# A two-layer decoder trunk on one core: output projection in one sum per chunk, sink-head biases on GpSimd, transposed probabilities of two key chunks in one bank

## The chip, the core and the metric

The kernel runs on one core of a Trainium2 chip. A core has five engines with their own instruction queues, each worked off strictly in order: TensorE (PE in the profile; its weight loads, PEld, overlap the matmuls), VectorE (DVE), ScalarE (ACT), GpSimd (POOL) and SyncE (SP, which only issues DMAs here). Engines wait for each other by semaphores. Matmul results land in PSUM, of which the kernel has eight banks of 128 x 512 float32; everything else lies in SBUF. The metric is the device time of one execution in microseconds (us).

## The reference

The input x is 512 tokens of 1024 numbers. All arithmetic is float32. Layer 0 mixes two kinds of attention heads, layer 1 has one kind, and each layer ends in a squared-ReLU MLP:

```python
def sliding_window_sink_attention(q, k, v, sinks, slopes):        # heads "B" of layer 0
    ...
    dist = qpos[:, None] - kpos[None, :] + BLOCK
    valid = ((dist >= 0) & (dist < WINDOW_B))[None] & (abs_k >= 0)[:, None, :]
    s = s - slope_kg * dist.astype(jnp.float32)
    s = jnp.where(valid[None, :, None, None], s, -jnp.inf)
    m = jnp.maximum(jnp.max(s, axis=-1, keepdims=True), sink)
    p = jnp.exp(s - m)
    den = jnp.sum(p, axis=-1) + jnp.exp(sink - m)[..., 0]
    ...
def even_mixer(...):
    ...
    y = jnp.concatenate([a_out.reshape(bsz, seq, -1), b_out.reshape(bsz, seq, -1)], axis=-1)
    return jnp.einsum("bse,ed->bsd", y, w_out)

def reference(x, ...):
    for layer in range(DEPTH):
        h = rms_norm(x, g_mix[layer])
        x = x + (even_mixer(h, ...) if layer % 2 == 0 else odd_mixer(h, ...))
        x = x + squared_relu_mlp(rms_norm(x, g_mlp[layer]), w_up[layer], w_down[layer])
    return x
```

Heads "A" of layer 0 (eight) mix three dilated windows; heads "B" (eight, in groups of four over two key heads) see the last 128 tokens and have a learned sink; heads "C" of layer 1 (sixteen) are causal with a forget gate. Head size is 64. After attention, the 16 heads side by side (1024 numbers per token) are multiplied by w_out (1024 x 1024) and added to x.

## The kernel before

**Tiling.** Float32 products are made of three fast ones: each operand is split into a high part and the rest (`split`, lines 147 to 156: high part by ACT, POOL or DVE, rest by DVE or POOL), and `mm3` (lines 163 to 169) multiplies high by high, low by high and high by low into one bank. Weights are loaded 512 KB at a time by SP into one of four buffers `wraw` (`load_w`, line 179) and then split into `whi` and `wlo`. The eight banks are two groups of four in rotation: `pA` for projections (`pj`) and the output projection (`op`), `pB` for all that attention does: transposed queries and keys (`qkT`), scores (`S`), transposed probabilities (`PT`) and head outputs (`O`). A buffer or bank is taken again only when its last reader is done, so a late reader makes a later writer wait.

**One head.** `scores` (lines 325 to 374) makes for each of the four blocks of 128 queries the scores of the keys in reach (PE, lines 348 and 349), adds the bias and takes the row's maximum (DVE, line 362), takes exponentials with their sum (ACT, line 365), the reciprocal of the sum (DVE, line 368), and scales the row (POOL, line 373, for three blocks, ACT, line 370, for the fourth). The bias of an A or B head is one DVE instruction per head, distance times slope plus a mask (lines 329 and 331; the tables `dist`, `lt`, `lb` are made at the start by `make_tables`, line 698). In a B head the sink goes as one more column into the row of probabilities (POOL copy, line 360). `values` (lines 376 to 410) transposes the probabilities by key chunk c = 0 to 3 on PE (line 385): chunk c holds the query blocks that see it, four, three, two and one of them for A and C heads, two, two, two and one for B heads. Each chunk has its own bank, from which ACT takes the high part (line 397) and DVE the rest (line 398). Chunks 2 and 3 share a tile `PT3`, in which 128 columns are zero so that chunk 3 can be multiplied at a width of 256. Then eight matmuls add the head's output up in one bank `O` (line 405), ACT and DVE add its two halves to `yf` (lines 408, 409), and behind every second head the pair's 128 rows are split into a tile y (line 156).

**What sets the order.** `run(att, n_att, dense, n_dense, lead)` (line 453) weaves a generator of attention steps with a generator of dense work, in proportion to `n_att` and `n_dense`. An attention step is one query block of `scores` or one step of `values` of the head before it; `values` had a step per key chunk and one for the output, so five. The tile framework then orders the instructions of each engine by what they wait for. Layer 0 has three such stages, at lines 566 to 569: two pairs of A heads with the projections for the B heads; the eight B heads with the projections for the other A heads; the other A heads with the output projection. Pairs are numbered as y tiles: A heads 0 to 3, B heads 4 to 7. Layer 1 has four stages (lines 596 to 599), the last with its output projection.

**The output projection** (`out_part`, lines 485 to 507) went over the eight chunks of 128 output columns with the pairs known first ([0, 1, 4, 5] in layer 0, twelve matmuls a chunk), added each bank to the residual (DVE, line 504, `acc<-op,xl`), then over the eight chunks again with the next pairs ([6, 7], six matmuls a chunk), adding to `acc` (`acc<-op,acc`), and a third time with the last two pairs inside the MLP's start (`finish`).

## Time and profile before

| | |
|---|---|
| three runs | 1161.77, 1161.94, 1162.87 us; median 1161.94 |
| the profiled execution | 1160.99 us, of which 1159.2 us from the first to the last instruction (the span) |
| busy, share of the span | PE 99%, PEld 84%, DVE 75%, ACT 56%, POOL 17% |
| granted TensorE clock | 1.000 |
| stages of layer 0 | heads A with projections about 45 to 100 us, heads B about 100 to 155, heads A with output projection about 155 to 215 |
| attention of layer 1 | about 605 to 812 us, the output projection from about 765 |
| MLPs | about 215 to 600 us and 812 us to the end |

The profile gives an instruction's start and end. Matmuls are pipelined: one starts before the end of the one ahead, and their ends are modelled, so PE looks busy almost all the time and short waits hide in it. A better reading is how many matmuls start in a stretch against how many could. A row of a group reads: line, engine, operation, what is written from what, shape, count, then busy us and mean ns of one, then idle time before them and what ended it.

### The profile page before, as it was taken

To read this page: it belongs to the slowest core of one execution; us is meant where nothing else is said; L and a number is where in the kernel's file an instruction comes from. 1 tells how busy PE (TensorE), PEld (TensorE's weight loads), DVE (VectorE), ACT (ScalarE), POOL (GpSimd) and SP (SyncE) were. 2 spreads that over 40 slices of the span, in tenths; PEclk is the share of its full clock that TensorE was granted. 3 is DMA by queue.
4 is the path that set the end of the run, shared out by engine and by line. 5 is a ranking of instruction groups with operands and counts; after the bars stand their busy time and mean duration, and the time that the engine had idled before them with its cause. 6 is when DMAs were issued, how large, how long until landed. Compare 5 with 4: busy or idle time off the path is not lost.

```text
span 1159.2 us, 17365 instructions
## 1 busy us (share of the span) xinstructions
PE 1141.9 (99%) x6228; PEld 977.8 (84%) x6228; DVE 873.0 (75%) x1865; ACT 645.2 (56%) x1342; POOL 198.1 (17%) x292
## 2 busy tenths in 40 slices
PE   9999999999999999999999999999999999999998
PEld 7887887888989988988988888888888888888887
DVE  7878899969868857855647877778858759669676
ACT  7555867655545455444335685655756455465452
POOL 0445434100000000000255545332100000000000
PEclk9999999999999999999999999999999999999999
DMA  8432114232333332433443433343420722523403
GB/s 288 131 91 74 55 38 146 75 108 91 93 108 92 112 105 76 123 96 111 147 128 109 110 101 98 111 129 117 161 86 18 230 80 67 188 73 111 147 34 109
DMA packets 94695, 126.57 MB, mean 109 GB/s; under 512 B 5888, under 2 KB 66304, under 8 KB 94608
## 3 DMA queue, kind: packets, MB, share of 16 engines
q1 hardware_dynamic: 93568, 123.29, 34.7%
q10 hardware_dynamic: 1040, 2.16, 0.5%
q8 instruction: 49, 0.80, 0.3%
q14 instruction: 38, 0.31, 0.1%
HBM read 114.39 MB, written 4.23 MB: 102 GB/s over the span
## 4 chain that ended last, share of the span: by engine, by line
PE 84%; DVE 8%; DMA 3%; ACT 2%; issue 2%; POOL 1%; SPq 0%; POOLq 0%; DVEq 0%; ACTq 0%
PE up L165 10%; PE up L169 10%; PE up L168 10%; PE pj L236 4%; PE pj L234 4%; PE pj L235 4%; PE O L405 3%; PE PT L385 2%; PE op L169 2%; PE op L165 2%; PE op L168 2%; PE Y L1045 2%; PE Y L1042 2%; PE Y L1044 2%; PE Y L1091 1%
## 5 line engine op out<-in xcount | busy, mean ns | idle before, releaser
L165 PE MATMUL up<-xin,whi 128*128 128x512 f32 x512 | 200.6, 392 | 0.0
L169 PE MATMUL up<-xin,whi 128*128 128x512 f32 x512 | 199.4, 389 | 0.0
L168 PE MATMUL up<-xin,wlo 128*128 128x512 f32 x512 | 199.3, 389 | 0.0
L791 ACT CAST whi<-wraw 128x512 fp32r<-128x512 f32 x228 | 139.2, 619 | 105.1 <-PE up L169 47.7
L792 DVE TENSOR_TENSOR wlo<-wraw,whi 128x512 fp32r<-128x512 f32 x228 | 151.6, 685 | 50.9 <-ACT whi L791 50.7
L169 PEld LDWEIGHTS up<-xin,whi 128*128 128x128 f32 x512 | 96.1, 188 | 20.1
L168 PEld LDWEIGHTS up<-xin,wlo 128*128 128x128 f32 x512 | 96.2, 188 | 19.9 <-issue 0.2
L165 PEld LDWEIGHTS up<-xin,whi 128*128 128x128 f32 x512 | 96.2, 188 | 19.6 <-issue 0.2
L365 ACT ACTIVATE P<-P,negm 128x128 f32<-128x128 f32 (+5 forms) x128 | 69.5, 543 | 42.7 <-DVE negm L362 40.3
L973 ACT ACTIVATE u<-up 128x512 f32<-128x512 f32 x64 | 38.3, 598 | 90.9 <-PE up L169 90.9
L234 PE MATMUL pj<-whi,hn 128*128 128x512 f32 (+2 forms) x256 | 88.7, 347 | 0.0
L236 PE MATMUL pj<-whi,hn 128*128 128x512 f32 (+2 forms) x256 | 87.0, 340 | 0.0
L235 PE MATMUL pj<-wlo,hn 128*128 128x512 f32 (+2 forms) x256 | 86.9, 339 | 0.0
L153 POOL TENSOR_SCALAR whi<-wraw 128x512 fp32r<-128x512 f32 x88 | 59.7, 680 | 158.7 <-PE pj L236 137.6
L812 DVE TENSOR_TENSOR t<-u 128x256 f32<-128x256 f32 x56 | 23.2, 423 | 62.8 <-ACT u L1116 61.1
L156 POOL TENSOR_TENSOR wlo<-wraw,whi 128x512 fp32r<-128x512 f32 x48 | 63.8, 1332 | 21.4 <-ACT whi L151 18.9
L156 DVE TENSOR_TENSOR wlo<-wraw,whi 128x512 fp32r<-128x512 f32 (+1 forms) x71 | 49.0, 698 | 18.6 <-POOL whi L153 15.1
L373 POOL TENSOR_SCALAR P<-P,rden 128x256 f32<-128x256 f32 (+2 forms) x96 | 48.0, 503 | 82.8 <-DVE rden L368 77.2
L397 ACT CAST PT<-PT 128x256 fp32r<-128x256 f32 (+3 forms) x128 | 48.9, 403 | 20.3 <-PE PT L385 19.4
L362 DVE CUSTOM_DVE_ANT_0 P<-S,bias 128x128 f32<-128x128 f32 (+1 forms) x96 | 45.7, 484 | 17.4 <-PE S L351 11.8
L791 ACT CAST whi<-mraw 128x512 fp32r<-128x512 f32 x64 | 38.8, 620 | 33.1 <-DVE mraw L902 14.4
L385 PE MATMUL PT<-ident,P 128*128 128x128 f32 x296 | 53.4, 276 | 2.4 <-DVE negm L362 1.4
(241 smaller groups left out, 3083.5 us busy)
## 6 DMA issues: line engine op xcount, KB each, us to landing
wraw<-in_w_up SPq DMA_DIRECT2D x64, 512.0 KB, 4.3
wraw<-in_w_down SPq DMA_DIRECT2D x56, 512.0 KB, 3.8
wraw<-in_w_in_odd SPq DMA_DIRECT2D x22, 512.0 KB, 3.8
wraw<-in_w_in_even SPq DMA_DIRECT2D x17, 512.0 KB, 5.0
mraw<-in_w_down SPq DMA_DIRECT2D x16, 512.0 KB, 4.7
K<-K SPq DMA_DIRECT2D x26, 256.0 KB, 2.9
bias<-csp SPq DMA_DIRECT2D x16, 256.0 KB, 3.3
wraw<-in_w_out_odd SPq DMA_DIRECT2D x8, 512.0 KB, 3.7
```

Source lines behind the costliest of these rows:

```text
L153: nc.gpsimd.tensor_scalar(dst_h, src, 1.0, 1.0, op0=OP.mult, op1=OP.mult)
L156: in_order((nc.gpsimd if lo == "pool" else nc.vector).tensor_sub(dst_l, src, dst_h.bitcast(F32)))
L165: m = nc.tensor.matmul(o, wh, xh, start=start, stop=False, skip_group_check=more)
L168: nc.tensor.matmul(o, wl, xh, start=False, stop=False, skip_group_check=more)
L169: nc.tensor.matmul(o, wh, xl, start=False, stop=stop, skip_group_check=more)
L234: nc.tensor.matmul(o, xh, hi[:, :n], start=k == 0, stop=False)
L235: nc.tensor.matmul(o, xh, lo[:, :n], start=False, stop=False)
L236: nc.tensor.matmul(o, xl, hi[:, :n], start=False, stop=k == DC - 1)
L365: nc.scalar.activation(p[:, :ne], p[:, :ne], AF.Exp, scale=-1.0, bias=negm[:, i:i + 1], accum_out=den[:, i:i + 1])
L385: nc.tensor.transpose(pt[:, (i - c) * P:(i - c + 1) * P], pr[i][:, kb * P:(kb + 1) * P], ident)
L791: sca(nc.scalar.copy(dst_h, src))
L792: late.append(lambda: vec(nc.vector.tensor_sub(dst_l, src, dst_h.bitcast(F32))))
```

## The change

Three edits, and new step counts for `run` where the number of steps changed.

First, `out_two` takes the place of the first two passes of the output projection: a chunk's bank takes the products of the first pairs (`a`), stays open, takes those of the next pairs (`b`), and is then added once to the residual. `OUT_ORDER` writes the order out by hand: four chunks' `a` first, with the loads of the residual (`x`) between, then their `b`, then chunk by chunk. The four `pA` banks are all open at the start of this.

Second, the masks of the B heads go into one float32 table of distances `db` (distance, and 1e30 where a key is out of reach), and a head's bias is that table times a number, by GpSimd.

Third, `values` puts two key chunks into one bank: (0, 1) and (3, 2) for B heads, 512 and 384 columns; 0, 1 and (3, 2) for A and C heads, 512, 384 and 384 columns. One ACT and one DVE instruction serve the two. The transposes and the matmuls are the same ones.

```diff
+OUT_ORDER = (("a", 0), ("a", 1), ("a", 2), ("x", 0), ("a", 3), ("b", 0), ("x", 2), ("b", 1), ("b", 2), ("b", 3), ("a", 4),
+             ("x", 4), ("b", 4), ("a", 5), ("b", 5), ("a", 6), ("x", 6), ("b", 6), ("a", 7), ("b", 7))
...
-NB = 86
+NB = 69
...
                 elif kind == "b":
-                    nc.vector.scalar_tensor_tensor(bias[:, :256], dist[:, 256:], -8.0 * float(slopes[h]), lb,
-                                                   op0=OP.mult, op1=OP.add)
+                    nc.gpsimd.tensor_scalar(bias[:, :256], db, -8.0 * float(slopes[h]), 1.0, op0=OP.mult, op1=OP.mult)
...
-                pts = []
-                for c in range(NT):
+                pts = {}
+
+                for cs in (((0, 1), (3, 2)) if kind == "b" else ((0,), (1,), (3, 2))):
                     pt = bank("pB", "PT")
...
-                    nc.scalar.copy(dst[:, 0], pt[:, :n])
-                    nc.vector.tensor_sub(dst[:, 1], pt[:, :n], dst[:, 0].bitcast(F32))
-                    pts.append((rhs, cols))
+                    nc.scalar.copy(d[:, 0], pt[:, :n])
+                    nc.vector.tensor_sub(d[:, 1], pt[:, :n], d[:, 0].bitcast(F32))
                     yield
...
+            def out_two(pa, pb):
...
+                for what, c in OUT_ORDER:
+                    if what == "x":
+                        xls[c // 2] = wp.tile([P, 2, 512], F32, tag="wraw", bufs=RAW, name="xl")
+                        nc.sync.dma_start(xls[c // 2], residual(li, c // 2))
+                        accs.append(acc_slot(f"acc{li}_{c // 2}"))
+                        continue
+                    if what == "a":
+                        os[c] = bank("pA", "op")
+                        product(c, pa, True, False)
+                        yield 32 * len(pa)
+                    else:
+                        product(c, pb, False, True)
+                        nc.vector.tensor_add(accs[c // 2][:, c % 2], os[c], xls[c // 2][:, c % 2])
+                        yield 32 * len(pb)
...
-                run(att_a(0), 32, chain(kv_b(), project([(1536, 2048)], qk_use("b", 8))), 768, LEADS[0])
+                run(att_a(0), 30, chain(kv_b(), project([(1536, 2048)], qk_use("b", 8))), 768, LEADS[0])
                 run(att_b(), NB, chain(qk_a(1), v_a(1)), 768, LEADS[1])
-                run(chain(att_a(1), last_values()), 38, chain(out_part([0, 1, 4, 5], True),
-                                                              out_part([6, 7], False), ahead([2, 3])), 1536, LEADS[2])
+                run(chain(att_a(1), last_values()), 33, chain(out_two([0, 1, 4, 5], [6, 7]), ahead([2, 3])), 1536, LEADS[2])
...
-                    run(att_c(g), 36, chain(qk_c(g + 1), v_c(g + 1)), 768, LEADS[3 + g])
-                run(chain(att_c(3), last_values()), 42, chain(out_part([0, 1, 2, 3], True),
-                                                              out_part([4, 5], False), ahead([6, 7])), 1536, LEADS[6])
+                    run(att_c(g), 32, chain(qk_c(g + 1), v_c(g + 1)), 768, LEADS[3 + g])
+                run(chain(att_c(3), last_values()), 37, chain(out_two([0, 1, 2, 3], [4, 5]), ahead([6, 7])), 1536, LEADS[6])
...
-        in_order(nc.vector.tensor_scalar(f[:, :256], dist[:, 256:], 0.0, -8.0 * BIG, op0=OP.is_lt, op1=OP.mult))
+        in_order(nc.vector.tensor_scalar(f[:, :256], dist[:, 256:], 0.0, BIG, op0=OP.is_lt, op1=OP.mult))
         yield
-        in_order(nc.vector.tensor_scalar(lb, dist[:, 256:], 128.0, -8.0 * BIG, op0=OP.is_ge, op1=OP.mult))
+        in_order(nc.vector.tensor_scalar(db, dist[:, 256:], 128.0, BIG, op0=OP.is_ge, op1=OP.mult))
         yield
-        in_order(nc.vector.tensor_add(lb, lb, f[:, :256]))
+        in_order(nc.vector.tensor_add(db, db, f[:, :256]))
+        yield
+        in_order(nc.vector.tensor_add(db, db, dist[:, 256:]))
         yield
```

The instructions also stand in another order. Three places matter below; numbers in names tell tiles of one kind apart, and line numbers are those of each kernel's own file (in the changed one the subtraction from a `PT` bank is line 404, the sum into `yf` line 414, the sum into `acc` line 518, the bias on GpSimd line 333).

**DVE at the end of the B heads**, where the sixth B head's output is summed into `yf` and the queries of the other A heads are normalised (`qk<-qk,rs`). Before:

```order
L331 SCALAR_TENSOR_TENSOR bias_2011<-dist_100,lb_102 128x256
L135 SCALAR_TENSOR_TENSOR rs_1862<-rsq_1868,rsq_1867 128x32 [waits DVE_49]
L161 SCALAR_TENSOR_TENSOR v0_103<-pj0_1885,rcol_95,v0_103 128x4x64
L275 TENSOR_TENSOR qk_1842<-qk_1842,rs_1862 128x512 [waits DVE_49]
L275 TENSOR_TENSOR qk_1843<-qk_1843,rs_1862 128x512
L409 TENSOR_TENSOR yf_1647<-O_1997,yf_1647 64x512 [waits Activation_49]
L362 ISA P_2019,negm_2013<-S_2016,bias_2011,nsink_86 128x128 [waits Pool_49]
```

In the changed kernel:

```order
L414 TENSOR_TENSOR yf_1615<-O_1944,yf_1615 64x512 [waits Activation_49]
L135 SCALAR_TENSOR_TENSOR rsq_1811<-ssv_1804,rsq_1810 128x32 [waits DVE_49]
L369 RECIPROCAL rden_1962<-den_1961 128x1 [waits Activation_49]
L363 ISA P_1987,negm_1960<-S_1984,bias_1958,nsink_86 128x256 [waits PE_49]
L363 ISA negm_1960 128x1
L136 TENSOR_TENSOR rsq_1811<-rsq_1811,rsq_1810 128x32 [waits DVE_49]
L404 TENSOR_TENSOR PT_1998<-PT_1993,PT_1998 128x512 [waits Activation_49]
L137 SCALAR_TENSOR_TENSOR rs_1805<-rsq_1811,rsq_1810 128x32 [waits DVE_49]
L158 TENSOR_TENSOR y0_6_1955<-yf_1615,y0_6_1955 128x512 [waits Activation_49]
L277 TENSOR_TENSOR qk_1785<-qk_1785,rs_1805 128x512 [waits DVE_49]
L277 TENSOR_TENSOR qk_1786<-qk_1786,rs_1805 128x512
```

The sum into `yf` now stands nine rows ahead of the two normalisations, and not behind them.

**DVE behind the second pair of A heads' keys**, in the stage with the output projection. Before, between the pair's last key and its first scores (`P<-S`):

```order
L301 TENSOR_TENSOR Q_2447<-qkT_2442,Q_2447 64x512 [waits Activation_49]
L329 SCALAR_TENSOR_TENSOR bias_2597<-dist_100,lt_101 128x512 [waits DVE_49]
L161 SCALAR_TENSOR_TENSOR K_2461<-qkT_2452,gg_85,K_2461 64x512 [waits DMAHW6_49,Activation_49]
L504 TENSOR_TENSOR acc0_2_2427<-op_2487,xl_2425 128x512 [waits PE_49]
L156 TENSOR_TENSOR wlo_2629<-wraw_2626,whi_2628 128x512 [waits DMAHW3_49,Pool_49]
L156 TENSOR_TENSOR wlo_2633<-wraw_2626,whi_2632 128x512 [waits Pool_49]
L504 TENSOR_TENSOR acc0_3_2545<-op_2546,xl_2543 128x512 [waits DMAHW2_49,PE_49]
L362 ISA P_2474,negm_2468<-S_2471,bias_2466 128x128 [waits PE_49]
```

In the changed kernel:

```order
L163 SCALAR_TENSOR_TENSOR K_2352<-qkT_2347,gg_85,K_2352 64x512 [waits DMAHW0_49,Activation_49]
L303 TENSOR_TENSOR Q_2342<-qkT_2337,Q_2342 64x512 [waits Activation_49]
L518 TENSOR_TENSOR acc0_0_2306<-op_2169,xl_2304 128x512 [waits PE_49]
L163 SCALAR_TENSOR_TENSOR K_2356<-qkT_2347,gg_85,K_2356 64x512 [waits DMAHW6_49,Activation_49]
L518 TENSOR_TENSOR acc0_0_2306<-op_2228,xl_2304 128x512 [waits PE_49]
L518 TENSOR_TENSOR acc0_1_2393<-op_2257,xl_2391 128x512 [waits DMAHW3_49,PE_49]
L518 TENSOR_TENSOR acc0_1_2393<-op_2307,xl_2391 128x512 [waits PE_49]
L363 ISA P_2386,negm_2380<-S_2383,bias_2378 128x128 [waits PE_49]
```

Two splits of weights (`wlo`) are gone from in front of the scores, and the sums into `acc` are four instead of two.

**GpSimd in the B heads.** Before:

```order
L360 COPY P_1928<-nsink_86 128x1 [waits PE_49,Pool_49]
L156 TENSOR_TENSOR wlo_2337<-wraw_2329,whi_2336 128x512 [waits Pool_49]
L373 TENSOR_SCALAR P_1754<-P_1754,rden_1750 128x128 [waits DVE_49]
L373 TENSOR_SCALAR P_1763<-P_1763,rden_1750 128x256 [waits DVE_49]
L360 COPY P_1955<-nsink_86 128x1 [waits PE_49]
L360 COPY P_1970<-nsink_86 128x1 [waits PE_49]
L373 TENSOR_SCALAR P_1790<-P_1790,rden_1750 128x256 [waits DVE_49]
```

In the changed kernel:

```order
L374 TENSOR_SCALAR P_1715<-P_1715,rden_1711 128x128 [waits DVE_49]
L361 COPY P_1911<-nsink_86 128x1 [waits PE_49,Pool_49]
L361 COPY P_1938<-nsink_86 128x1 [waits PE_49,Activation_49]
L374 TENSOR_SCALAR P_1724<-P_1724,rden_1711 128x256 [waits DVE_49]
L158 TENSOR_TENSOR wlo_2262<-wraw_2258,whi_2261 128x512 [waits DMAHW5_49,Activation_49]
L333 TENSOR_SCALAR bias_1958<-db_102 128x256 [waits DVE_49]
L374 TENSOR_SCALAR P_1753<-P_1753,rden_1711 128x256 [waits DVE_49]
```

A head's bias now stands between the scalings of the rows of the head before it, here behind a split of output weights that waits for its load (DMAHW5) and for ScalarE.

More of the change, by code (lines that the diff above doesn't have):

```diff
@@ L376, in values, with blocks @@
             def values(pr, kind, V, vs, yf, j):
[L378 to L379 removed]
+                def blocks(c):
+                    return [i for i in range(c, NT) if kind != "b" or i <= c + 1]
+                pts = {}
+                for cs in (((0, 1), (3, 2)) if kind == "b" else ((0,), (1,), (3, 2))):
                     pt = bank("pB", "PT")
[L381 to L399 removed]
@@ new lines, in values @@
+                    n = 0
+                    for c in cs:
+                        for i in blocks(c):
+                            kb = c - (max(i - 1, 0) if kind == "b" else 0)
+                            nc.tensor.transpose(pt[:, n:n + P], pr[i][:, kb * P:(kb + 1) * P], ident)
+                            n += P
+                    if cs == (3, 2):
+                        d = p3[:, :, P:]
+                        pts[3] = p3[:, :, :256], slice(256, 512)
+                        pts[2] = p3[:, :, 256:], slice(256, 512)
+                    else:
+                        d = ap.tile([P, 2, 512 - cs[0] * P], F32R, tag=f"PT{cs[0]}", bufs=1, name="PT")
+                        o = 0
+                        for c in cs:
+                            m = len(blocks(c)) * P
+                            pts[c] = d[:, :, o:o + m], slice(c * P, c * P + m)
+                            o += m
@@ L483, in out_weights, with product, out_last @@
                 return load_w(runs, w, np_, PAT_OP)
-            def out_part(pairs, first, finish=None, tiles=None):
+            def out_two(pa, pb):
+                ws, xls, os = {}, {}, {}
+                def product(c, pairs, start, stop):
+                    w = 1024 // len(pairs)
+                    c0 = c // (w // P) * (w // P)
+                    if (len(pairs), c0) not in ws:
+                        ws[len(pairs), c0] = out_weights(pairs, c0)
+                    cw = slice((c - c0) * P, (c - c0 + 1) * P)
+                    for kk, n in enumerate(pairs):
+                        hi, lo = ws[len(pairs), c0][kk]
+                        mm3(os[c], hi[:, cw], lo[:, cw], ys[n][:, 0], ys[n][:, 1], start and kk == 0,
+                            stop and kk == len(pairs) - 1)
+                for what, c in OUT_ORDER:
[12 more added lines that the diff above has]
+                        yield 32 * len(pb)
+            def out_last(pairs, finish, tiles):
                 np_ = len(pairs)
                 w = 1024 // np_
-                tiles = tiles or {}
                 for c in range(DC):
@@ L495, in out_part @@
                     cw = slice(e * P, (e + 1) * P)
-                    if first and c % 2 == 0:
-                        xl = wp.tile([P, 2, 512], F32, tag="wraw", bufs=RAW, name="xl")
-                        nc.sync.dma_start(xl, residual(li, c // 2))
-                        accs.append(acc_slot(f"acc{li}_{c // 2}"))
                     o = bank("pA", "op")
@@ L503, in out_part @@
                     a = accs[c // 2][:, c % 2]
-                    nc.vector.tensor_add(a, o, xl[:, c % 2] if first else a)
-                    if finish is not None:
-                        finish(c, a)
+                    nc.vector.tensor_add(a, o, a)
+                    finish(c, a)
                     yield 32 * np_
@@ L696, in start, with make_tables @@
             pass
-    def make_tables(ap, dist, lt, lb):
+    def make_tables(ap, dist, lt, db):
         def scratch(dt, tag, name):
```

23 lines of the change are left out of this document (4 added, 19 removed).

## The prediction

> **What bounds the kernel now.** I read the page's head first, then busy time by stage, then what PE waited for, and the rows around each of those waits.
>
> ```profile
> PE 1141.9 (99%) x6228; PEld 977.8 (84%) x6228; DVE 873.0 (75%) x1865; ACT 645.2 (56%) x1342; POOL 198.1 (17%) x292
> ```
>
> Busy time by stage (columns: the stretch, its length, busy us and instructions of PE, PEld, DVE, ACT, POOL, the clock, DMA):
>
> ```profile
> 45.00:100.00 55.00, 54.27 (x313) 46.31 (x312) 42.94 (x131) 32.14 (x82) 24.43 (x38) 1.00 0.31 90
> 100.00:155.00 55.00, 52.84 (x350) 45.35 (x350) 48.67 (x163) 41.95 (x122) 29.08 (x64) 1.00 0.18 53
> 155.00:215.00 60.00, 56.20 (x306) 46.77 (x305) 54.39 (x136) 37.12 (x93) 21.27 (x29) 1.00 0.36 106
> 605.00:765.00 160.00, 158.13 (x994) 136.51 (x993) 124.00 (x344) 98.72 (x235) 74.62 (x96) 1.00 0.37 106
> 900.00:928.90 28.90, 28.90 (x129) 23.96 (x128) 20.53 (x33) 12.63 (x23) 0.00 (x0) 1.00 0.72 229
> ```
>
> PE is the bound; the change keeps every matmul, so only its waits can be won. The last row, an MLP stretch at full flow, holds some 128 matmuls of 512 columns: 28.90 / 128 = 0.226 us each. One is shown longer than that:
>
> ```profile
> L168 PE MATMUL up<-xin,wlo 128*128 128x512 f32 x512 | 199.3, 389 | 0.0
> ```
>
> So a wait below about 0.16 us does not show, and one that shows is about 0.16 us longer than shown (0.389 - 0.226). In 100 to 215 us PE stands idle for 2.16 + 3.80 us, and there DVE is busy 103.1 of 115 us, 90%. In layer 1's attention PE idles 1.9 us. What PE waited for from 45 to 215 us (in total, times, longest):
>
> ```profile
> PE PT L385 <- DVE negm L362: 1.4, 1, 1.4
> PE S L348 <- DVE yf L409: 1.2, 1, 1.2
> PE qkT L290 <- DVE qk L275: 1.2, 2, 0.7
> PE qkT L290 <- POOL qk L275: 1.1, 2, 0.5
> PE PT L385 <- POOL P L373: 0.9, 1, 0.9
> PE O L405 <- DVE PT L398: 0.4, 2, 0.3
> PE op L169 <- DVE y L156: 0.3, 1, 0.3
> PE S L348 <- DVE Q L301: 0.2, 1, 0.2
> PE O L405 <- ACT PT L397: 0.2, 1, 0.2
> ```
>
> Together 6.9 us, nearly all behind DVE. The two kinds at `qkT` (2.3 us) are the normalisation of queries; its instructions stay, and I leave them.
>
> **The change part by part.** The costs by shape (whole run):
>
> ```profile
> L397 ACT CAST PT<-PT 128x512 fp32r<-128x512 f32 x24 | 14.0, 584 | 5.9 <-PE PT L385 5.6
> L398 DVE TENSOR_TENSOR PT<-PT 128x512 fp32r<-128x512 f32 x24 | 16.4, 685 | 0.4 <-ACT PT L397 0.4
> L398 DVE TENSOR_TENSOR PT<-PT 128x384 fp32r<-128x384 f32 x24 | 13.2, 550 | 0.4 <-ACT PT L397 0.2
> L398 DVE TENSOR_TENSOR PT<-PT,PT 128x256 fp32r<-128x256 f32 x32 | 13.2, 414 | 0.1
> L398 DVE TENSOR_TENSOR PT<-PT,PT 128x128 fp32r<-128x128 f32 x32 | 8.9, 279 | 1.7 <-ACT PT L397 1.7
> L331 DVE SCALAR_TENSOR_TENSOR bias<-dist,lb 128x256 f32<-128x256 f16 x8 | 3.7, 461 | 0.0
> L504 DVE TENSOR_TENSOR acc<-op,acc 128x512 f32<-128x512 f32 x32 | 21.7, 682 | 2.9 <-PE op L169 2.6
> L373 POOL TENSOR_SCALAR P<-P,rden 128x256 f32<-128x256 f32 x40 | 20.9, 524 | 10.9 <-DVE rden L368 10.5
> ```
>
> Two chunks per bank: an A or C head takes 0.414 + 0.279 - 0.550 = 0.143 us less of DVE, a B head 3 x 0.414 + 0.279 - 0.685 - 0.550 = 0.286 us less. ACT is relieved in the same way; at 56% busy nothing of the sum is put on it. One sum: of the 32 `acc<-op,acc`, 16 fall away (8 per layer, 0.682 us each, 5.5 us of DVE per layer). Biases: 8 x 0.461 = 3.7 us leave DVE. In 100 to 155 us DVE thus loses 2.3 + 3.7 = 6.0 of 48.67 us, in 155 to 215 us 5.5 + 0.6 = 6.1 of 54.39: 12%. None of it is PE time as such; it counts where PE waited behind DVE. Four waits are in places that the new order alters.
>
> *The sum into `yf`.* The rows of DVE and PE around 156 us:
>
> ```profile
> 153.26 2.81 DVE L275 TENSOR_TENSOR qk<-qk,rs 128x512 f32<-128x512 f32 x2
> 156.10 0.68 DVE L409 TENSOR_TENSOR yf<-O,yf 64x512 f32<-64x512 f32 x1
> 156.84 0.39 PE L348 MATMUL S<-K,Q 128*128 128x256 f32 x1 [1.23 <-DVE yf L409]
> ```
>
> A score needs the bank that `yf` still reads, and `yf` stands behind two normalisations. By the new order it stands nine rows ahead of them: 1.2 + 0.16 = 1.4 us go. Late next is the second half of `PT`, behind the normalisations now; PE has 20 projection matmuls between the two parts of that head's output to fill it.
>
> *The scores of the second pair.* DVE first, then PE:
>
> ```profile
> 187.43 2.12 DVE L156 TENSOR_TENSOR wlo<-wraw,whi 128x512 fp32r<-128x512 f32 x2
> 189.48 0.68 DVE L504 TENSOR_TENSOR acc<-op,xl 128x512 f32<-128x512 f32 x1
> 190.08 0.27 DVE L362 CUSTOM_DVE_ANT_0 P<-S,bias 128x128 f32<-128x128 f32 x1
> 190.41 0.55 PE L385 MATMUL PT<-ident,P 128*128 128x128 f32 x3 [1.41 <-DVE negm L362]
> ```
>
> The transposes need a bank that the first score still holds, and its maximum stands behind two splits and a sum, 2.7 us of DVE. The splits no longer stand there; the last of the four sums there needs 0.68 us after its matmuls, which the head's own score matmuls cover in good part. 1.4 + 0.16 = 1.6 us go.
>
> *The weights of the second quarter.* GpSimd:
>
> ```profile
> 172.53 1.13 POOL L153 TENSOR_SCALAR whi<-wraw 128x512 fp32r<-128x512 f32 x1 [1.35 <-DMA wraw<-in_w_out_even]
> 173.63 0.93 POOL L373 TENSOR_SCALAR P<-P,rden 128x384 f32<-128x384 f32 x2
> ```
>
> GpSimd waited for a load of output weights, with a head's scalings queued behind; that is PE's 0.9 us at the scaling. `OUT_ORDER` asks for these weights before the first residual, so one 512 KB load earlier on SP: 1.0 us goes.
>
> *The last y.* The output projection waited 0.3 us for the pair split last; with `b` of the last chunk and more matmuls on the pair before it, 13 instead of 10 matmuls stand in between, 0.7 us more. 0.3 + 0.16 = 0.5 us go.
>
> The short waits at `O` and `Q` (0.8 us shown, four times 0.16 hidden, and, as an estimate, as much again too short to show) come to 2.9 us; with 12% less DVE I take a quarter, 0.7 us. Layer 1's attention has 1.9 us shown, and of that
>
> ```profile
> PE S L348 <- DMA K<-K: 1.7, 2, 1.2
> ...
> K<-K SPq DMA_DIRECT2D x26, 256.0 KB, 2.9
> ```
>
> is the copy of a key's halves, which stays; from the rest and from 45 to 100 us I take 0.5 us.
>
> What is added. (1) Eight biases on GpSimd: the scaling of the same size, 0.524 us, eight times 4.2 us in a stage where it is busy 29.08 of 55. At nothing, since a head's bias is made while the head before it is at work; without that cover, up to 0.524 us each. (2) One more addition of 256 columns in the tables, 0.414 us at most, in the first 45 us: 0.2. (3) In the first A head of the output stage no matmuls of the projection stand between the seven transposes, the scores and the first output product: between the first four transposes and that product PE has three transposes and two scores, about 1.1 us, against 0.584 + 0.685 us of ACT and DVE and a maximum on DVE before it: between 0 and 1.6, taken 0.8 for being nearer such a wait than not. (4) Between a pair's keys and its first scores lie 26 and 24 output matmuls (5.9 and 5.4 us) where about 27 and 24 lay; the copy takes 2.9 us after DVE's part: 0 to 1.2, taken 0.3.
>
> Sum: 1.4 + 1.6 + 1.0 + 0.5 + 0.7 + 0.5 = 5.7 off, 0.2 + 0.8 + 0.3 = 1.3 on, net 4.4 us off. The profiled execution took 1160.99 us (1159.2 of span and 1.8 around it), 0.95 under the median of the runs: 1156.6 there, 1157.5 against 1161.94.
>
> [...] DVE from 45 to 215 us, and the same split in the MLPs, where GpSimd is idle:
>
> ```profile
> L156 DVE TENSOR_TENSOR wlo<-wraw,whi 128x512 fp32r<-128x512 f32 x17 | 13.0, 767 | 1.3 <-POOL whi L153 1.2
> L156 DVE TENSOR_TENSOR y<-yf,y 128x512 fp32r<-128x512 f32 x8 | 6.3, 782 | 0.8 <-ACT y L151 0.7
> L275 DVE TENSOR_TENSOR qk<-qk,rs 128x512 f32<-128x512 f32 x4 | 4.9, 1276 | 0.0
> L792 DVE TENSOR_TENSOR wlo<-wraw,whi 128x512 fp32r<-128x512 f32 x228 | 151.6, 685 | 50.9 <-ACT whi L791 50.7
> ```
>
> Beside a working GpSimd these take 17 x 0.082 + 8 x 0.097 + 4 x 0.59 = 4.5 us longer, over 74.8 us of GpSimd: 0.06 us per us, so 0.25 us of DVE for 4.2 us more. [...]
>
> **The rivals.**
>
> *Waits come back elsewhere* (1161): each wait removed shows the next dependency; on a PE that stalls only some 10 us from 45 to 215 us the scheduler's new order may hold as many. For it: at (3) and (4) I can name two. Against: DVE, the common releaser, has 12% less to do. 4.4 us off, 3.5 back.
>
> [...]
>
> *GpSimd's queue becomes the late one* (1165, the slower side): in the B heads the biases stand between sink copies, scalings and a split that waits for its load; a head's scalings then come late, and its transposes with them. It decides when most of the eight push a scaling that PE waits for: 8 x 0.524 = 4.2 on, and the DVE gain of that stage gone: 1161.94 + 4.2 - 1.0. For it: PE's 0.9 us behind a GpSimd scaling at 173 us. Against: GpSimd is busy 53% there.
>
> **How the numbers follow.** Forecast 1157.5: 0.64; waits come back 0.18; DVE held off 0.06; GpSimd's queue 0.12. A measurement here tells 0.2%, 2.3 us, from no change. Faster takes nearly all of the forecast and a sixth of the two middle cases: 0.66; same 0.21; slower 0.13. The forecast's own range is 1153 to 1159.6: the 5.7 with no addition and 3 us more of waits that do not show, or the 5.7 with the additions' upper ends (0.4 + 1.6 + 1.2 = 3.2). The whole range, 1151 to 1164, takes in the middle cases and leaves most of the last out.
>
> **What would show it.** Right: no wait of PE for `yf` or for the maximum above 0.5 us in 100 to 215 us, DVE about 12 us less busy up to 215 us, the MLP starting some 4 us earlier, layer 1 within 1 us of before. Wrong: a wait of PE for `O` behind `PT` or for `K` of 1 us or more in the output stage; GpSimd as releaser of transposes in the B heads; `wlo` on DVE well above 767 ns.

## The result and the profile after

The changed kernel takes 1172.89 us (median; 1171.91 to 1174.94) against 1162.01 us (1161.77 to 1162.87): a ratio of 1.0098, 95% interval 1.0086 to 1.0109. It is 10.9 us slower; the forecast was 4.4 us faster, and the range of the prediction (1151 to 1164) does not hold it.

The profiled execution took 1171.91 us with a span of 1170.1. Its busy line, then what PE waited for in the whole span (in total, times, longest):

```profile
PE 1147.0 (98%) x6228; PEld 977.7 (84%) x6228; DVE 860.4 (74%) x1802; ACT 643.9 (55%) x1302; POOL 204.9 (18%) x300
```

```profile
PE O L410 <- DVE PT L404: 4.8, 6, 1.7
PE S L349 <- DMA K<-K: 2.9, 3, 1.2
PE qkT L292 <- DVE qk L277: 2.2, 2, 1.6
```

The matmuls are the same 6228, and DVE is busy 12.6 us less, on 63 instructions fewer. What is new is the first wait: the output product for the rest of the transposed probabilities, 4.8 us where it was 0.4.

**Where the time went.** A comparison by clock time does not line the two kernels up, so I lined them up by work: every matmul is counted at its undisturbed start-to-start time in these traces (0.227 us for 512 columns, 0.176 for 384, 0.120 for 256, 0.108 for a transpose), and for an amount of work the table gives the time at which a kernel gets there, less that of before. A rising number is lost PE time, and the place where it rises is the place of the loss. All kernels of the experiments stand in it but two sets of leads (further, small steps). The six added matmuls of one kernel count as work here, so that kernel loses 1.4 us more than its row says.

| work done, us (before is there at) | 80 (89) | 110 (124) | 140 (158) | 200 (222) | 650 (679) | 690 (720) | 730 (760) | 800 (832) |
|---|---|---|---|---|---|---|---|---|
| the changed kernel | 2.0 | 4.2 | 3.9 | 4.5 | 5.7 | 7.0 | 9.4 | 10.9 |
| biases alone | 0.9 | 0.8 | 2.5 | 0.4 | 0.3 | 0.3 | 0.3 | 0.2 |
| one sum alone | 0.3 | 0.3 | 0.3 | 0.0 | 0.0 | 0.0 | 0.1 | 2.6 |
| pairs alone | 0.4 | 2.7 | 3.0 | 1.9 | 3.2 | 4.5 | 8.3 | 8.4 |
| pairs undone | 0.7 | 0.7 | 2.3 | 1.4 | 2.2 | 2.2 | 2.2 | 4.0 |
| pairs, empty steps behind | 0.5 | 3.1 | 2.6 | 5.4 | 5.9 | 6.9 | 6.6 | 6.7 |
| pairs, empty steps ahead | 1.4 | 3.3 | 1.9 | 1.3 | 2.2 | 3.1 | 4.9 | 5.0 |
| two chunks a step | 1.1 | 1.3 | 0.3 | 0.1 | 1.0 | 0.7 | 5.1 | 5.4 |
| six more matmuls | 3.1 | 3.7 | 3.2 | 3.0 | 5.9 | 7.2 | 11.1 | 12.7 |
| changed, leads u | 1.9 | 1.6 | 3.4 | 0.1 | 3.8 | 4.9 | 4.9 | 5.4 |
| changed, leads v | 0.7 | 2.6 | 3.4 | 1.0 | 3.1 | 3.5 | 6.3 | 7.1 |
| changed, leads w | 2.2 | 2.2 | 2.6 | 2.8 | 10.2 | 11.1 | 11.3 | 15.7 |
| before, leads 0.03 up | 1.3 | 0.6 | 1.8 | 1.1 | 2.5 | 3.1 | 8.2 | 9.0 |
| before, leads 0.03 down | -0.1 | 1.0 | 4.4 | 4.6 | 10.9 | 11.0 | 14.6 | 14.8 |
| changed, leads by stage | 0.5 | 0.2 | 1.4 | -0.3 | 1.2 | 2.2 | 2.2 | 3.0 |
| changed, leads by stage, 2nd | 1.1 | 2.0 | 3.2 | 1.7 | 2.6 | 3.4 | 3.4 | 3.9 |

So the changed kernel loses 4.5 us in layer 0, 1.9 of it on the way into the B heads (work 80 to 100), nothing in the MLPs, and 6.4 us in layer 1's attention, 2.2 of it around one wait of its third stage. These two places show what happens in the others too.

*The third stage of layer 1*, around 759 us. All engines, rows in between left out:

```profile
755.29 1.29 POOL L158 TENSOR_TENSOR wlo<-wraw,whi 128x512 fp32r<-128x512 f32 x1
...
755.33 1.29 DVE L133 TENSOR_SCALAR rsq<-rsqb 128x32 int32<-128x32 int32 x1
...
757.44 0.16 DVE L369 RECIPROCAL rden<-den 128x1 f32<-128x1 f32 x1
...
757.63 0.72 ACT L371 ACTIVATE P<-P,rden 128x512 f32<-128x512 f32 x1 [1.37 <-DVE rden L369]
...
758.26 0.46 ACT L403 CAST PT<-PT 128x384 fp32r<-128x384 f32 x1
...
758.69 2.14 DVE L277 TENSOR_TENSOR qk<-qk,rs 128x512 f32<-128x512 f32 x2
...
760.75 0.55 DVE L404 TENSOR_TENSOR PT<-PT,PT 128x384 fp32r<-128x384 f32 x1
761.35 0.62 PE L410 MATMUL O<-PT,v 128*128 128x256 f32 x3 [1.72 <-DVE PT L404]
```

Read it from below. The product waits 1.72 us for the last subtraction, which stands in DVE's queue behind two normalisations of queries (2.14 us). What it subtracts, ACT's copy, was ready at 758.72, just as they began. Both came late: DVE was held up at 755.33, where an instruction of 128x32 elements took 1.29 us and ended with GpSimd's split, and the reciprocal that ACT waited for stands behind it. The kernel before was held up in that chain as well (1.13 us, beside a split of GpSimd from 746.83 to 748.12), and yet PE did not wait, since the last subtraction of that head stood ahead of the normalisations. So the order makes the difference here, as the experiments on the order below bear out:

```profile
747.01 1.13 DVE L268 TENSOR_SCALAR ssv<-ss,ecol 128x8 f32<-128x8 f32 x1
...
751.42 0.28 DVE L398 TENSOR_TENSOR PT<-PT,PT 128x128 fp32r<-128x128 f32 x1
...
752.29 2.14 DVE L275 TENSOR_TENSOR qk<-qk,rs 128x512 f32<-128x512 f32 x2
```

*The way into the B heads*, around 102 us. DVE, GpSimd and PE of the changed kernel:

```profile
101.40 1.17 DVE L136 TENSOR_TENSOR rsq<-rsq 128x32 f32<-128x32 f32 x1
102.60 0.19 DVE L137 SCALAR_TENSOR_TENSOR rs<-rsq 128x32 f32<-128x32 f32 x1
102.83 2.14 DVE L277 TENSOR_TENSOR qk<-qk,rs 128x512 f32<-128x512 f32 x2
```

```profile
101.25 1.28 POOL L158 TENSOR_TENSOR wlo<-wraw,whi 128x512 fp32r<-128x512 f32 x1
```

```profile
103.67 0.30 PE L292 MATMUL qkT<-ident,qk 128*128 128x128 f32 x1 [1.63 <-DVE qk L277]
...
107.48 0.63 PE L236 MATMUL pj<-whi,h 128*128 128x512 f32 x1
```

Again an instruction in a chain of small DVE instructions takes about a microsecond more beside a split of GpSimd (1.17 us, the next one 0.19), and ends 0.05 us behind it. PE then waits 1.63 and 0.51 us, little more in all than before (0.65, 0.51 and 0.55 us), but with less work in between. In the next microseconds a matmul of 512 columns, shown as 0.39 us elsewhere, takes 0.63. The granted clock (the column ahead of the DMA share) tells why:

```profile
103.00:104.00 1.00, 0.30 (x1) 0.14 (x1) 1.00 (x2) 0.00 (x0) 1.00 (x1) 1.00 0.78 180
...
106.00:107.00 1.00, 1.00 (x3) 0.86 (x4) 0.00 (x0) 0.56 (x1) 0.00 (x0) 0.50 0.00 0
...
109.00:110.00 1.00, 1.00 (x10) 0.99 (x10) 0.95 (x4) 0.41 (x2) 0.19 (x1) 1.00 0.00 0
```

It was halved from 104.7 to 108.1 us, 3.41 us, which costs up to half of that in work, 1.7 us: by this estimate most of the 1.9 us lost here. While PE was at work, before never had it under 1.00.

### The profile page after: what moved, and what is told of

It is laid out like the page before. It is cut to its first block, busy times and chain, and to the rows that moved or that the text cites. A ratio compares the mean times of both kernels' runs of the same rounds, so it can differ in the third digit from the quotient of the medians.

```text
span 1170.1 us, 17305 instructions
## 1 busy us (share of the span) xinstructions
PE 1147.0 (98%) x6228; PEld 977.7 (84%) x6228; DVE 860.4 (74%) x1802; ACT 643.9 (55%) x1302; POOL 204.9 (18%) x300
## 4 chain that ended last, share of the span: by engine, by line
PE 78%; DVE 9%; DMA 4%; ACT 3%; issue 3%; POOL 2%; SPq 0%; POOLq 0%; ACTq 0%; DVEq 0%
PE up L167 10%; PE up L171 10%; PE up L170 10%; PE pj L238 3%; PE pj L236 3%; PE pj L237 3%; PE O L410 2%; PE op L171 2%; PE Y L1076 2%; PE Y L1073 2%; PE Y L1075 2%; PE op L170 2%; PE op L167 2%; DVE wlo L158 2%; PE Y L1122 1%
## 5 line engine op out<-in xcount | busy, mean ns | idle before, releaser
L410 PE MATMUL O<-PT,v 128*128 128x256 f32 (+2 forms) x256 | 55.3, 331 | 6.8 <-DVE PT L404 4.8
L410 PEld LDWEIGHTS O<-PT,v 128*128 128x128 f32 x256 | 41.0, 188 | 19.4 <-DVE PT L404 8.8
L822 ACT CAST whi<-mraw 128x512 fp32r<-128x512 f32 x64 | 38.8, 619 | 33.1 <-DVE mraw L933 14.4
```

What stands on the lines that cost most here:

```text
L410: nc.tensor.matmul(po[:, cols], V[:, c, vs], rhs[:, part], start=n_ == 0 and part == 0, stop=n_ == 3 and part == 1, skip_group_check=True)
L822: sca(nc.scalar.copy(dst_h, src))
```

## Experiments

### One edit at a time

The kernel before with one edit each, and the changed kernel with the paired banks undone. The edits are those of the diff above; the step counts go with the pairs:

```diff
 biases alone:  the bias of B heads by GpSimd from db, and db in make_tables
 one sum alone: out_part -> out_two, out_last, OUT_ORDER
 pairs alone:   values() of the changed kernel;
-               run(att_a(0), 32  NB = 86  ... 38  run(att_c(g), 36  ... 42
+               run(att_a(0), 30  NB = 69  ... 33  run(att_c(g), 32  ... 37
 pairs undone:  the changed kernel with values() and the step counts of before
```

> The kernel before with one of the three edits: the biases of the B heads by GpSimd from the table db. The changed kernel is 10.9 us slower than before; where its TensorE work falls behind, counted at equal work done, is 0.8 us in the first 36 us, 0.7 at 50 us, 2.4 at the passage from A heads to B heads (102 to 108 us) and 6.5 us in layer 1's attention, where this edit changes nothing. Theory P (the paired banks make the loss): within 2 us of before, 1160 to 1163. Theory G (GpSimd's queue): 1165 or more, the stall at 102 to 108 us here too. Theory J (the parts only hurt together): 1159 to 1163.

> The kernel before with one edit: the output parts in one sum, in the order of OUT_ORDER; PT per chunk and the old step counts. Theory P: faster by the two waits that the prediction removed in the output stage, 1158 to 1161; layer 1's attention up to its output stage as before. Theory S (one sum of six heads' pairs holds banks and asks weights in another order, and that costs): slower by 2 to 4 us, all of it after 155 us in layer 0 and after 765 us in layer 1. Theory J: 1158 to 1162.

> The kernel before with one edit: the transposed probabilities of two chunks in one bank, with the step counts of the changed kernel (30, 69, 33; 32, 37). Theory P: most of the loss is here, 1167 to 1173, with waits of TensorE at O for the DVE half of PT of 3 us or more in total, two of them over 1 us between 695 and 765 us, where this kernel and the changed one have the same instructions. Theories G and S: 1160 to 1164. Theory J: 1160 to 1166.

> The changed kernel with one part undone: PT per chunk again, with the step counts of before (32, 86, 38; 36, 42); one sum and the biases on GpSimd stay. Theory P: the forecast's own ground, 1157 to 1162, no wait of O for PT above 0.5 us. Theories G and S: 1165 to 1173. Theory J (the parts only hurt together): 1158 to 1164, as each part alone.

Measured, against 1161.01 us of before: biases 1162.36 (ratio 1.0011, 1.0001 to 1.0020), one sum 1163.58 (1.0018, 1.0009 to 1.0028), pairs 1169.68 (1.0072, 1.0057 to 1.0087), pairs undone 1166.16 (1.0042, 1.0027 to 1.0057).

The three alone add up to 1.4 + 2.6 + 8.7 = 12.6 us, about the whole loss of 10.9, so they do not need each other to hurt. The pairs make most of it, as theory P said; with the biases alone it is 1.3 us (0.1 to 2.3). But theory P expected the one sum to win and the kernel with the pairs undone to be level, and both are slower; theory S named the one sum's loss (2 to 4 us), theory G's 1165 us for the biases alone did not come. In layer 0 the one sum gains 1.7 us between work 160 and 170, which the table steps over, where before waited 1.4 us behind a maximum, and gives 1.2 us of it back by 200. That gain is not shown to be its own: biases alone and pairs alone gain 1.6 us at the same place and two chunks a step (next section) 1.2, all three with the output projection of before. In layer 1's output stage it loses 2.6 us at waits that before did not have there (755 to 825 us, the kernel with one sum alone):

```profile
PE S L350 <- DMA K<-K: 1.0, 1, 1.0
PE S L350 <- DVE acc L515: 0.7, 1, 0.7
PE op L171 <- DVE y L158: 0.3, 1, 0.3
```

The kernel with pairs alone shows the waits at O of the changed kernel:

```profile
PE O L409 <- DVE PT L403: 3.9, 5, 1.7
```

and its clock fell twice, on the way into the B heads (0.50 from 104 to 106 us) and behind the stall of the third stage:

```profile
758.00:760.00 2.00, 1.15 (x5) 1.15 (x6) 0.94 (x3) 0.10 (x1) 1.82 (x2) 0.67 0.00 0
760.00:762.00 2.00, 2.00 (x11) 2.00 (x10) 1.20 (x2) 0.88 (x2) 0.00 (x0) 0.50 0.00 0
```

That is why this stage costs 3.6 us there (4.7 to 8.3 between work 720 and 730) and 2.2 us in the changed kernel, whose clock held there at 1.00.

### The step, the width or the pacing

With two chunks in one bank three things change at once: the last piece of a head is 384 columns wide where it was 128; it comes one step ahead of the product where chunk 2 came two; and with fewer steps per head every attention step lands at another place of the projection. Two kernels have the pairs, with empty steps that give each head the steps of before, behind the last bank or ahead of it; a third has the instructions of before in the steps of the changed kernel:

```diff
 empty steps behind / ahead (all step counts as before; None is an empty step)
-for cs in (((0, 1), (3, 2)) if kind == "b" else ((0,), (1,), (3, 2))):
+for cs in (((0, 1), (3, 2), None, None) if kind == "b" else ((0,), (1,), (3, 2), None)):
+for cs in ((None, (0, 1), None, (3, 2)) if kind == "b" else ((0,), (1,), None, (3, 2))):
 two chunks a step (values() of before, step counts 30, 69, 33; 32, 37)
-    yield
+    if c == 3 or c == 1 or (c == 0 and kind != "b"):
+        yield
```

> The kernel before with the paired banks, but with empty steps in each head's values (one for A and C heads, two for B heads) behind the last bank and ahead of the output product, so that the step counts of before (32, 86, 38; 36, 42) hold and every other piece of work stands where it stood. Pairs alone with the new step counts measured 8.4 us slower. Theory R (it is the new pacing that puts other work in the way): 1159 to 1163, no wait of O for PT over 0.5 us. Theory D (it is the lost step between the last transposes and the product): 1159 to 1163 too, the same sign, since the step is given back. Theory W (it is the wider copy and subtraction as such): 1163 to 1167, the waits at O still there, shorter.

> As the run with empty steps behind the last bank, but the empty steps stand ahead of it: the same number of steps and the pacing of before, the last bank (384 columns) directly one step ahead of the product. Theory R: 1159 to 1163, as with the empty steps behind. Theory D and theory W: 1164 to 1169, with waits of O for the DVE half of PT of 2 us or more in total.

> The kernel before with a bank, a copy and a subtraction per chunk as before, but two chunks in one step, and the step counts of the changed kernel (30, 69, 33; 32, 37): its pacing with the narrow instructions of before. Theory R: 1167 to 1171, as pairs alone, 1169.7. Theory D: 1164 to 1169, since the last two chunks now come in the last step. Theory W: 1160 to 1163.

Measured, against 1161.05: behind 1168.31 (1.0068, 1.0053 to 1.0083), ahead 1165.70 (1.0042, 1.0027 to 1.0057), two a step 1166.31 (1.0043, 1.0026 to 1.0059).

No theory passes in all three kernels: R fits none, D the second and the third, W the second. Pacing alone is not it (the pacing of before, with the pairs, loses 4.7 and 7.3 us), nor the width alone (narrow instructions lose 5.3), nor the lost step (given back between the last bank and the product, it loses the most of the three). The table shows why the sums mislead: each kernel loses at other places. With the steps behind, the stall of the third stage is gone (6.9 to 6.6), and in layer 0's output stage a wait of 3.2 us for a copy of keys comes instead (work 160 to 170); DVE's part of those keys stands behind a split there. With narrow instructions nothing is lost up to layer 1, and the third stage loses 4.4 us, up to 1.7 of it by a fall of the clock (755.26 to 758.68 us). The order is that of the changed kernel, though only 128 columns are behind the normalisations (DVE, then PE):

```profile
753.09 2.14 DVE L275 TENSOR_TENSOR qk<-qk,rs 128x512 f32<-128x512 f32 x2
755.16 0.28 DVE L398 TENSOR_TENSOR PT<-PT,PT 128x128 fp32r<-128x128 f32 x1
```

```profile
755.49 0.58 PE L406 MATMUL O<-PT,v 128*128 128x256 f32 x1 [1.90 <-DVE PT L398]
```

So the size of the piece hardly matters there: behind the normalisations the wide one cost a wait of 1.72 us and the narrow one of 1.90. With the empty steps behind, the wide piece is done ahead of them (755.50 against 758.73 us), and the wait is gone. What counts is the side of the normalisations on which it falls. That suggested theory O, that the order itself decides and any shift costs.

### Does an idle PE halve the clock?

The changed kernel with six more matmuls, whose result the transposes overwrite, at the place where PE waited on the way into the B heads:

```diff
 def head_T(qk, off, fill=0):
     pt = bank("pB", "qkT")
+    for _ in range(fill):
+        nc.tensor.matmul(pt, hT[0][:, 0, :P], hT[0][:, 0, :], start=True, stop=True)
 ...
-    return prep_q(st["qk", "b"], p_ * P), [k, k]
+    return prep_q(st["qk", "b"], p_ * P, 0 if p_ else 6), [k, k]
```

> The changed kernel with six more matmuls (128x512, 1.36 us of TensorE, their result overwritten by the transposes that follow) ahead of the first query transposes of the B heads, where TensorE stood idle 1.6 and 0.5 us and the granted clock then fell to 0.5 for 3.41 us. Theory H (the clock falls because TensorE did too little work, 0.95 us of 3.41, before it): no fall of the clock there, and 1.7 us less than the changed kernel: 1171 against 1172.9. Theory N (the clock falls for another reason): the fall stays, 1172.5 to 1174.

Measured: 1174.14 us (1.0112, 1.0097 to 1.0127). The clock held there, as theory H said:

```profile
102.00:104.00 2.00, 1.44 (x7) 0.74 (x5) 1.90 (x5) 0.00 (x0) 0.99 (x1) 1.00 1.11 318
104.00:106.00 2.00, 0.94 (x5) 0.50 (x4) 1.10 (x1) 0.00 (x0) 2.00 (x3) 1.00 0.55 121
```

The changes of the clock lie multiples of 3.41 us apart in the traces (last section), and by stretches of that length the two executions can be compared: the one in question ran here from 101.35 to 104.77 us and held 1.9 us of work, 1.36 of it the added matmuls; in the changed kernel it ran from 101.28 to 104.69 and held 0.95. Between work 80 and 100 this kernel lost nothing against before beyond the 1.36 us of those matmuls, where the changed kernel lost 1.9 us. But in this execution the clock fell at 46.7 and at 763.5 us, behind stalls that the changed kernel has too and where its clock held. So the time is no better, and it lies in neither theory's range: the stalls were still there, and like stalls brought a fall in one execution and none in the other (below).

### Other leads

Theory O can be tried without touching an instruction. `LEADS` says by how much a stage's attention steps run ahead of its dense work. Three other sets for the changed kernel, and one for the kernel before, each lead up by 0.03, about one attention step (in the B heads, with 86 steps, between two and three):

```diff
-LEADS = (0.0, 0.0, -0.16, 0.33, -0.3, -0.23, -0.09)
+LEADS = (0.05, 0.03, -0.12, 0.3, -0.36, -0.26, -0.05)    changed kernel, u
+LEADS = (-0.05, -0.03, -0.2, 0.36, -0.27, -0.29, -0.13)  changed kernel, v
+LEADS = (0.08, 0.06, -0.24, 0.24, -0.42, -0.32, 0.0)     changed kernel, w
+LEADS = (0.03, 0.03, -0.13, 0.36, -0.27, -0.2, -0.06)    kernel before, up
```

> The changed kernel with other leads, by which a stage's attention steps run ahead of its dense work: (0.05, 0.03, -0.12, 0.3, -0.36, -0.26, -0.05) for (0, 0, -0.16, 0.33, -0.3, -0.23, -0.09); all instructions stay. Theory O (the loss is a matter of where the last PT subtraction stands in VectorE's queue, by the pacing): with -0.26 the subtraction of the last head of layer 1's third stage stands ahead of the two normalisations and not behind them, and with -0.36 ahead of the sums of squares in the second stage; so the waits at O of 1.2 and 1.9 us there go, and layer 1 loses about 3 us less than in the changed kernel; the others are open, in all 1167 to 1172. Theory W (two chunks in one bank are late wherever they stand): the waits at O stay, 3 us or more in layer 1, and 1171 to 1175.

> The changed kernel with the leads (-0.05, -0.03, -0.2, 0.36, -0.27, -0.29, -0.13). Theory O: with -0.29 the wait of 1.9 us at O in layer 1's third stage goes; in the second stage (-0.27) the subtraction still stands behind a row maximum, so that wait of 1.2 us stays at least in part; 1169 to 1174. Theory W: both stay, 1171 to 1175.

> The changed kernel with leads further off: (0.08, 0.06, -0.24, 0.24, -0.42, -0.32, 0). Theory O: each stage's loss comes out anew, by up to 3 us either way, since the order decides it; 1165 to 1178. Theory W: the loss by stage is as in the changed kernel within 1 us, 1171 to 1175.

> The kernel before, nothing of the change, with each lead 0.03 higher, about one attention step: (0.03, 0.03, -0.13, 0.36, -0.27, -0.2, -0.06). Theory O: the kernel before loses from a shift of one step as the changed one does, by waits at O, K and the transposes that it has not now: 1164 to 1172. Theory W: narrow instructions bear the shift, 1160 to 1163.

Measured, against 1161.33: u 1166.48 (1.0052, 1.0035 to 1.0069), v 1168.61 (1.0063, 1.0048 to 1.0078), w 1175.05 (1.0119, 1.0104 to 1.0134), and the kernel before with its leads up 1170.17 (1.0078, 1.0063 to 1.0094). Theory W's ranges hold none of the four, w by a hair. Theory O's hold the last two; u and v come out 0.5 and 0.4 us under them.

The last is the finding of this study. Without any of the change, a shift of about one step costs 8.8 us, as much as the pairs. Over half of it (5.1 us between work 690 and 730) goes at the same place by the same order, up to 1.7 of that by a fall of the clock from 758.55 to 761.96 us. DVE of that kernel, with the normalisations stretched to 2.87 us and the last 128 columns behind them, and PE's wait from 740 to 765 us:

```profile
755.78 2.87 DVE L275 TENSOR_TENSOR qk<-qk,rs 128x512 f32<-128x512 f32 x2
758.57 0.28 DVE L398 TENSOR_TENSOR PT<-PT,PT 128x128 fp32r<-128x128 f32 x1
```

```profile
PE O L405 <- DVE PT L398: 2.5, 2, 2.2
```

Set u bears theory O out where it was definite: with -0.36 the last piece of the second stage stands ahead of three of the sums of squares, with -0.26 that of the third ahead of the normalisations, and between work 660 and 730 the kernel loses 0.9 us (4.0 to 4.9) where the changed one lost 3.5 (5.9 to 9.4). DVE of set u in the third stage:

```profile
753.84 0.54 DVE L404 TENSOR_TENSOR PT<-PT,PT 128x384 fp32r<-128x384 f32 x1
...
757.06 2.14 DVE L277 TENSOR_TENSOR qk<-qk,rs 128x512 f32<-128x512 f32 x2
```

In v, -0.29 was meant to mend the third stage too and did not: 2.8 us go there, at waits for ACT's copy and for DVE. Standing ahead of the normalisations is not enough when the chain before it is held up.

### Leads put together

The stages follow each other, so the leads of the stages that lost least can be joined. One such set, two sets that go on in some directions, a second joined set, and the kernel before with its leads down by 0.03:

```diff
+LEADS = (-0.05, 0.06, -0.12, 0.33, -0.27, -0.26, -0.05)  changed kernel, by stage
+LEADS = (-0.1, 0.1, -0.08, 0.42, -0.33, -0.26, -0.03)    changed kernel, further
+LEADS = (-0.03, 0.04, -0.14, 0.38, -0.24, -0.25, -0.07)  changed kernel, small steps
+LEADS = (-0.05, 0.06, -0.12, 0.38, -0.33, -0.26, -0.05)  changed kernel, by stage, 2nd
+LEADS = (-0.03, -0.03, -0.19, 0.30, -0.33, -0.26, -0.12) kernel before, down
```

> The changed kernel with the lead of each stage from the run in which that stage lost least: (-0.05, 0.06, -0.12, 0.33, -0.27, -0.26, -0.05). The stages' own losses against before, added up, are 0.4 + 0.4 - 3.2 + 1.3 + 0.4 + 0.0 + 0.5 = -0.2. Theory O (order alone decides, stages add up): 1159 to 1163, level with before. Theory W (the paired banks cost in any order, and the stages' gains do not add up): 1164 to 1168.

> The changed kernel with the leads (-0.1, 0.1, -0.08, 0.42, -0.33, -0.26, -0.03): tells what the stages do further along the direction that was better. Theory O: any stage may come out 1 us better or 3 us worse; 1160 to 1172. Theory W: 1165 to 1175.

> The changed kernel with the leads (-0.03, 0.04, -0.14, 0.38, -0.24, -0.25, -0.07): small steps about the better ones. Theory O: 1160 to 1170. Theory W: 1165 to 1172.

> The kernel before with each lead 0.03 lower, about one attention step to the other side: (-0.03, -0.03, -0.19, 0.3, -0.33, -0.26, -0.12). Theory O (before sits at a low point of its leads): slower here too, 1164 to 1171. Theory S (only one direction is bad, and another order would be better still): 1158 to 1162.

> The changed kernel with the leads (-0.05, 0.06, -0.12, 0.38, -0.33, -0.26, -0.05), two of them in layer 1 other than in the last set put together: with 0.38 that stage lost 0.8 us in the run that had it, with -0.33 the next lost 0.6. Theory O: 1162 to 1164.5, 0.5 to 2 us under the last set. Theory W: 1164 to 1167, since a stage's loss moves to the next.

Measured: by stage 1164.49 against 1161.67 (1.0025, 1.0016 to 1.0035), further 1170.50 (1.0071, 1.0056 to 1.0086), small steps 1167.56 (1.0044, 1.0029 to 1.0059); by stage, 2nd 1164.22 against 1161.64 (1.0024, 1.0015 to 1.0032), before with its leads down 1176.00 (1.0117, 1.0102 to 1.0133).

Seven numbers, and no instruction, take the changed kernel from 10.9 us behind to 2.8. All of its waits at O from 610 to 770 us are then

```profile
PE O L410 <- DVE PT L404: 0.4, 1, 0.4
```

and layer 0 ends level with before (-0.3). The kernel before loses to both sides, 8.8 us up and 14.4 down (four falls of the clock among the latter, up to 1.7 us each by the same estimate, and a mean clock of 0.994), so along this line, all seven leads together, it sits at a low point: the change was measured with an order that was right for other instructions. The stages do not quite add up (-0.2 forecast from their sums, 2.8 measured). The first joined set so falls in theory W's range (1164 to 1168) and not in theory O's, the second in both; why the sums miss was not looked into. No version here beats the kernel before. Whether the last 2.6 us are the edits' own price or an order not found stays open; so does which of the many small waits would go first.

## Why the prediction was wrong

**The step that failed** is the list of what is added. It held four things, each with a price, and not the one that counted: with two chunks in a bank and fewer steps per head, in all seven stages, the instructions of every head get another place among those of the projection. The prediction priced the waits that the trace of before showed and two that it could name; the rest of the order it took as kept, "layer 1 within 1 us of before". Layer 1's attention lost 6.4 us. The rival "waits come back elsewhere" had the right mechanism and gave it 3.5 us; from the forecast's 4.4 us off to the measured 10.9 on it is 15.3. Other leads alone take back 8 of the 10.9 us, so that much hangs on the order; how much of the new order comes from the wider pieces and how much from the steps stays open.

**What VectorE was relieved of** was sized right: summed over their instructions the sums into `acc` fell by 10.9 us, the subtractions by 5.6, the biases by 4.1 (forecast 10.9, 5.7 and 3.7). The sentence behind it, that it counts only where PE waited behind DVE, was right too. But the waits were not nearly all behind DVE: of the 6.9 us listed it was 4.7, and GpSimd had 2.0. The quarter of the short waits taken as a gain on account of 12% less work was not to be found.

**The sum into `yf`**, -1.4: that wait is 0.3 us now. But the subtraction that stands behind the normalisations instead was said to be covered by 20 projection matmuls, and it was not: the normalisations took 2.98 us beside GpSimd (DVE and PE).

```profile
157.33 2.98 DVE L277 TENSOR_TENSOR qk<-qk,rs 128x512 f32<-128x512 f32 x2
...
160.70 0.55 DVE L404 TENSOR_TENSOR PT<-PT,PT 128x384 fp32r<-128x384 f32 x1
```

```profile
161.30 0.85 PE L410 MATMUL O<-PT,v 128*128 128x256 f32 x5 [1.10 <-DVE PT L404]
```

The net gain at this place is 0.1 to 0.2 us. It was the very order that later cost most in layer 1, named for one head and not looked for in the others.

**The scores of the second pair** (-1.6) and **the weights of the second quarter** (-1.0): PE's 1.4 and 0.9 us there are gone, as forecast. The reasons given are not shown: both waits are gone with biases alone and with pairs alone too, which leave the output projection as it was. And a further wait at O in the output stage (1.03 us behind ACT's copy, at 196.7 us) ate most of the first. **The last y** (-0.5): the lost PE time there fell from 0.49 to 0.22 us in the changed kernel and grew to 0.76 with one sum alone.

**Added (1)**, the biases at nothing, and **(2)**, 0.2 for the tables: together 1.3 us measured, with an interval from 0.1 to 2.3. **(3)**, the first output product of the output stage behind PT, 0.8 out of 0 to 1.6: two waits of 0.3 us show at its place (170.9 and 172.2 us), and by the count of work about 1.4 us are lost there (work 147 to 150). **(4)**, the copies of K, 0.3 out of 0 to 1.2: in layer 0's output stage PE waits for none of them; their waits rose from 1.7 to 2.9 us elsewhere, at 56 us and in layer 1.

**The signs.** The waits for `yf` and for the maximum fell to 0.3 us, and DVE was 10.4 us less busy up to 215 us (182.7 to 172.4; 12 forecast), in part because the kernel was behind by then; the MLP started 4.5 us later all the same. Of the signs of being wrong one came, the wait of O behind PT in the output stage (1.03 us). Four waits and a relieved engine say little of the total as long as other waits can come.

**The rivals.** GpSimd's queue did not become late: no wait of PE names it in the B heads but the one at the normalised queries, which before had too. DVE held off by GpSimd, one of the two middle cases at 1161 and given 0.06: no run shows it. Beside the eight biases, of 0.40 to 0.85 us each in the changed kernel, DVE's instructions took 0.65 us more in all than the median of their kind. But the price of 0.06 us per us was an average over long instructions, and the average hid what happens in a chain of short ones; see below. The clock was taken as 1.00 throughout; it was not asked what a longer stall does to it.

## What to carry to other kernels

A kernel whose engines take their work in a fixed order, woven by numbers that were chosen for it, can sit at a low point of those numbers, as this one does along the line that was tried. An edit that alters the number of steps then moves everything, and its first measurement tells mostly the price of the lost order (here 8 of 11 us) rather than that of the edit. So choose the numbers anew before judging, measure the unchanged kernel with its numbers shifted as a scale for what a shift costs, and line traces up by work done, stage by stage, since the stages' gains and losses hide each other in the total. In the order, look for the long piece of a slow engine (here 2.14 us of normalisation) and for what falls behind it.

## What the runs showed of the hardware

**The granted clock.** In the traces of the kernel before and of the changed one the granted clock is 1.00 or 0.50. The record of the clock begins at 5.56 and 5.71 us, and to 0.01 us its changes lie multiples of 3.4133 us behind that and behind one another: 338 times before (1159.27 us), 29, 1 and 311 times in the changed kernel (104.69, 108.11 and 1169.65 us). Counted in stretches of that length, the clock fell behind three: in the changed kernel behind that from 101.28 to 104.69 us, in which matmuls and transposes made up 0.95 us of work, with waits of 1.63 and 0.51 us, and in each kernel behind the last whole one of the execution, where PE ran out of work (0 and 0.04 us). The 675 other stretches of full clock held 2.07 us of work or more before, 1.64 or more in the changed kernel, and the clock stayed at 1.00 behind each. The fall at 104.69 us costs, by the estimate above, up to 1.7 us. Like stalls did not always bring one: in the kernel with six more matmuls the clock fell at 46.7 and 763.5 us, where the changed kernel's stretches from 43.25 and 760.05 us held 1.64 and 2.03 us of work and its clock stayed at 1.00. What made the difference there is not shown.

**Small VectorE instructions beside GpSimd.** The reciprocal roots are a chain of DVE instructions of 128x32 elements. In the traces of the kernel before and of the changed one 115 of them started with no GpSimd instruction at work, or with under 0.06 us of one left, and none took more than 0.20 us. 17 started beside one: 11 of those took 0.31 to 1.29 us and ended 0.03 to 0.05 us behind that GpSimd instruction, the other six took 0.18 to 0.27 us, and one of these ended ahead of it. The DVE rows at 755.33 and 101.40 us above are two of the 11. An average over long instructions hides it, but such a meeting made a chain up to 1.1 us later here (1.29 against 0.19 us), and PE with it where it waited for that chain.
